# Rotary embedding, fp32: 64 rows of x to a partition, table halves made by TensorE and VectorE, x staged in PSUM by ScalarE

## Chip, cores, metric

One core of one Trainium2 chip. The metric is the device time of one execution in microseconds (us); lower is better. The *span* of a profile runs from the first to the last instruction that it shows. It is shorter than the measured time, that difference here called the **gap**.

## The reference

x is (8, 8, 1024, 64) in fp32, 16.8 MB; the tables are (1024, 32) each.

```python
half = x.shape[-1] // 2
x_first, x_second = x[..., :half], x[..., half:]
out_first  = x_first * cos_cached - x_second * sin_cached
out_second = x_first * sin_cached + x_second * cos_cached
return np.concatenate([out_first, out_second], axis=-1)
```

Each row needs two products over its 64 elements (by sin and by cos) and two sums over 32. Everything is read once and written once: 33.8 MB of transfers with the tables.

## The kernel before

x is cut into 16 chunks of 128 partitions x 32 rows (8 KB a partition). The tables lie in SBUF (for GpSimd) and in PSUM (for VectorE). VectorE makes the products of most chunks; the sums are made by GpSimd (`vector_pool`), by TensorE with the identity and its negative plus a copy back by ScalarE (`vector_tensor`), or by VectorE (`vector_alone`). Two chunks are GpSimd's alone.

```python
R = 32; F = R * hd; T = R * half; Q = seq // R        # 32 partitions hold one table
for first, n in [(0, 1), (1, 1)] + [(c, 2) for c in range(2, n_ch, 2)]:
    t = xp.tile([P, n, F], fp32, name=f"x{first}")    # all of x fits in SBUF
    nc.sync.dma_start(out=t, in_=xf[first:first + n].rearrange("c p m -> p c m"))
# ... identity `plus` on GpSimd, `minus` on ScalarE
for r in range(reps):                                 # tables to PSUM, four times
    nc.vector.tensor_copy(out=snp[r * Q:(r + 1) * Q], in_=sn[0:Q])
    nc.scalar.copy(out=csp[r * Q:(r + 1) * Q], in_=cs[0:Q])
for t in (sn, cs):                                    # and in SBUF for GpSimd
    for r in range(1, reps):
        nc.gpsimd.tensor_copy(out=t[r * Q:(r + 1) * Q], in_=t[0:Q])

def products(eng, c, s, ctab, stab):
    xr = rows(xt[c])
    eng.tensor_tensor(out=rows(s), in0=xr, in1=tab(stab), op=TT.mult)
    eng.tensor_tensor(out=xr, in0=xr, in1=tab(ctab), op=TT.mult)
# ... vector_tensor(0); on_pool(1); vector_pool(2); ... vector_alone(15)
```

## Time and profile before

| | before |
|---|---|
| measured time, median of 4 runs | 85.98 us (85.87 to 86.01) |
| span of the profile | 84.2 us |
| gap between time and span | 1.8 us |
| busy: VectorE, GpSimd, ScalarE | 84%, 85%, 19% of the span |
| moved | 33.82 MB in 4736 packets |

A kernel that is bound by its transfers gets faster only by moving its bytes more cheaply or by making the ramp and the tail shorter.

### The profile page before, as it was taken

What the parts mean: (1) busy time and instruction counts of PE and PEld (TensorE: products, weight loads), DVE (VectorE), ACT (ScalarE), POOL (GpSimd) and SP (SyncE); (2) the same over time, 40 slices, a digit from 0 to 9 for tenths busy, and PEclk for the clock granted to TensorE, in tenths of its full rate; (3) what the DMA queues carried; (4) which work ended last, traced back from release to release, by engine and by line L of the source; (5) the groups of instructions that cost most, each with busy time, mean ns of one, the idle gap of its engine ahead of it and who ended that gap; (6) DMA issues with size and microseconds to landing.
All of it is one profiled execution on the core that took longest, in us unless ns stands there. A gap on an engine that the chain in (4) does not pass through costs nothing.

```text
span 84.2 us, 363 instructions
## 1 busy us (share of the span) xinstructions
PE 40.1 (48%) x80; PEld 15.7 (19%) x80; DVE 70.4 (84%) x34; ACT 15.7 (19%) x16; POOL 71.4 (85%) x38
## 2 busy tenths in 40 slices
PE   0000005994930896895949497794949600000000
PEld 0000002422400341423314051332414100000000
DVE  0199997999999999999999982999999999996000
ACT  4399000004040003104040402204040310000000
POOL 3199999999999999999999999999999999970000
PEclk9999999999999569999999999999999999555555
DMA  3899999999999999999999999999999999999991
GB/s 29 282 432 409 420 420 436 417 409 420 436 428 409 417 428 432 432 424 409 421 436 436 432 421 417 424 424 436 432 432 432 413 421 428 428 436 407 432 419 55
DMA packets 4736, 33.82 MB, mean 402 GB/s; under 512 B 448, under 2 KB 448, under 8 KB 768
## 3 DMA queue, kind: packets, MB, share of 16 engines
q1 hardware_dynamic: 3824, 27.40, 78.7%
q10 hardware_dynamic: 912, 6.42, 18.1%
HBM read 17.04 MB, written 16.78 MB: 402 GB/s over the span
## 4 chain that ended last, share of the span: by engine, by line
POOL 53%; DVE 23%; issue 9%; DMA 4%; DVEq 1%; POOLq 0%
POOL x L94 13%; POOL x L93 11%; DVE vs L88 11%; POOL x L89 11%; POOL gs L88 11%; DVE x L89 8%; POOL sn L77 4%; DMA sn<-in_sin_cached_dram 4%; POOL cs L77 3%; DVE acc L88 3%; DVE x L93 1%; DVEq L170 1%; POOLq L93 0%; POOLq L77 0%
## 5 line engine op out<-in xcount | busy, mean ns | idle before, releaser
L119 PE MATMUL acc<-x,plus 128*128 128x512 f32 x40 | 23.3, 666 | 26.4 <-DVE x L89 13.6
L89 DVE TENSOR_TENSOR x<-x,csp 128x2048 f32<-128x2048 f32 x14 | 32.0, 2287 | 0.6
L88 DVE TENSOR_TENSOR vs<-x,snp 128x2048 f32<-128x2048 f32 x13 | 29.7, 2282 | 2.2 <-POOL x L94 1.7
L122 ACT COPY x<-acc 128x1024 f32<-128x1024 f32 x10 | 10.1, 1012 | 49.2 <-PE acc L120 49.2
L94 POOL TENSOR_TENSOR x<-x,vs 128x1024 f32<-128x1024 f32 (+1 forms) x9 | 19.0, 2108 | 0.0
L93 POOL TENSOR_TENSOR x<-x,vs 128x1024 f32<-128x1024 f32 (+1 forms) x9 | 18.9, 2105 | 0.0
L119 PEld LDWEIGHTS acc<-x,plus 128*128 128x128 f32 x40 | 7.5, 208 | 39.4 <-issue 23.9
L120 PE MATMUL acc<-vs,minus 128*128 128x512 f32 x20 | 11.6, 666 | 0.0
L120 PE MATMUL acc<-vs,plus 128*128 128x512 f32 x20 | 10.2, 592 | 0.0
L89 POOL TENSOR_TENSOR x<-x,cs 128x2048 f32<-128x2048 f32 x2 | 9.1, 4546 | 0.2
L88 POOL TENSOR_TENSOR gs<-x,sn 128x2048 f32<-128x2048 f32 x2 | 9.1, 4542 | 0.1
L73 DVE COPY snp<-sn 32x1024 f32<-32x1024 f32 x4 | 4.9, 1223 | 3.9 <-DMA sn<-in_sin_cached_dram 3.8
L120 PEld LDWEIGHTS acc<-vs,minus 128*128 128x128 f32 x20 | 4.4, 219 | 5.9 <-issue 5.9
L77 POOL COPY sn<-sn 32x1024 f32<-32x1024 f32 x3 | 3.1, 1032 | 2.7 <-DMA sn<-in_sin_cached_dram 2.6
L93 POOL TENSOR_TENSOR x<-x,gs 128x1024 f32<-128x1024 f32 x2 | 4.7, 2362 | 0.2
L94 POOL TENSOR_TENSOR x<-x,gs 128x1024 f32<-128x1024 f32 x2 | 4.7, 2357 | 0.0
L120 PEld LDWEIGHTS acc<-vs,plus 128*128 128x128 f32 x20 | 3.8, 190 | 4.8 <-issue 4.8
L74 ACT COPY csp<-cs 32x1024 f32<-32x1024 f32 x4 | 4.0, 1008 | 1.5 <-DMA cs<-in_cos_cached_dram 1.4
L77 POOL COPY cs<-cs 32x1024 f32<-32x1024 f32 x3 | 3.1, 1033 | 0.1
L88 DVE TENSOR_TENSOR acc<-x,snp 128x2048 f32<-128x2048 f32 x1 | 2.3, 2297 | 0.0
L71 ACT ACT_TABLE_LOAD x1 | 1.3, 1283 | 1.2 <-PEq L159 1.2
L93 DVE TENSOR_TENSOR x<-x,acc 128x1024 f32<-128x1024 f32 x1 | 1.2, 1223 | 0.0
(8 smaller groups left out, 2.4 us busy)
## 6 DMA issues: line engine op xcount, KB each, us to landing
x<-in_x_dram SPq DMA_DIRECT2D x7, 2048.0 KB, 25.0
out_dram<-x SPq DMA_DIRECT2D x9, 1024.0 KB, 13.0
out_dram<-x ACTq DMA_DIRECT2D x6, 1024.0 KB, 9.0
x<-in_x_dram SPq DMA_DIRECT2D x2, 1024.0 KB, 6.3
out_dram<-x SPq DMA_DIRECT2D x2, 512.0 KB, 6.0
cs<-in_cos_cached_dram ACTq DMA_DIRECT2D x1, 128.0 KB, 3.4
sn<-in_sin_cached_dram SPq DMA_DIRECT2D x1, 128.0 KB, 3.1
```

What stands on the lines that cost most here:

```text
L71: nc.scalar.mul(minus, plus, -1.0)
L73: nc.vector.tensor_copy(out=snp[r * Q:(r + 1) * Q], in_=sn[0:Q])
L74: nc.scalar.copy(out=csp[r * Q:(r + 1) * Q], in_=cs[0:Q])
L77: nc.gpsimd.tensor_copy(out=t[r * Q:(r + 1) * Q], in_=t[0:Q])
L88: eng.tensor_tensor(out=rows(s), in0=xr, in1=tab(stab), op=TT.mult)
L89: eng.tensor_tensor(out=xr, in0=xr, in1=tab(ctab), op=TT.mult)
L93: eng.tensor_tensor(out=xr[:, :, 0], in0=xr[:, :, 0], in1=sr[:, :, 1], op=TT.subtract)
L94: eng.tensor_tensor(out=xr[:, :, 1], in0=xr[:, :, 1], in1=sr[:, :, 0], op=TT.add)
L119: nc.tensor.matmul(a[:, k], plus, xr[:, :, k], start=True, stop=False)
L120: nc.tensor.matmul(a[:, k], plus if k else minus, sr[:, :, 1 - k], start=False, stop=True)
L122: nc.scalar.copy(out=xr, in_=a.rearrange("p k n j -> p n k j"))
L170: with _tile.TileContext(nc) as tc:
```

## The change

The intent: longer contiguous runs of x (16 KB a partition) in fewer and larger transfers, and less table work at the start. With 64 rows to a partition, a partition needs table rows of two neighbouring blocks of 32. The even blocks are spread over 128 partitions by a selection matrix on TensorE; the odd ones are shuffled by VectorE into 32 partitions and copied to the rest. From the second half of unit 0 on, the tables lie in SBUF only, so ScalarE copies x to PSUM ahead of VectorE's products, which keeps VectorE at one SBUF input.

```diff
-    R = 32
+    R = 64                                   # F and T double; 8 units, not 16 chunks
+    for m0, m1 in ((0, F // 2), (F // 2, F)):
+        nc.sync.dma_start(out=xt[0][:, m0:m1], in_=xf[0][:, m0:m1])
+    for u in range(1, n_u):
+        nc.sync.dma_start(out=xt[u], in_=xf[u])             # 16 KB a partition
...
-    for r in range(reps):
-        nc.vector.tensor_copy(out=snp[r * Q:(r + 1) * Q], in_=sn[0:Q])
-        nc.scalar.copy(out=csp[r * Q:(r + 1) * Q], in_=cs[0:Q])
+        for i in range(2):                                  # even blocks
+            for part, r in zip(even, (rs, rc)):
+                nc.tensor.matmul(part[i], sel, r[:, i * BK:(i + 1) * BK], start=True, stop=True)
+        odd = [2 * (i % (Q // 2)) + 1 for i in range(Q)]    # odd blocks
+        for t, r in ((sn, rs), (cs, rc)):
+            nc.vector.stream_shuffle(t[0:Q, C:], r, odd)
+        # ... three copies each on ScalarE and GpSimd; even blocks copied to SBUF by ScalarE
...
+    def stage(pt, u, n0, n1):
+        nc.scalar.copy(out=pt[:, :(n1 - n0) * hd], in_=xt[u][:, n0 * hd:n1 * hd])
+    def products(pt, u, n0, n1, alone=False):
+        mul(nc.vector, sr, pr, tab(sn, n0, n1))             # pr: x in PSUM
+        mul(nc.vector, pr if alone else xr, pr, tab(cs, n0, n1))
...
+    # unit 2 is GpSimd's; units 1, 3 to 7 go in chunks of 24, 24 and 16 rows:
+    for c, (u, n0, n1) in enumerate(chunks):
+        products(st[c % 2], u, n0, n1, (u, n0) in alone)
+        put(c + 2)                                          # stage two chunks ahead
+        # ... TensorE's sums back, next TensorE sums, GpSimd's sums, stores of whole units
```

## The prediction

> **What bounds the kernel now.** I read three views in this order: the strip of 40 slices, the table of busy time in chosen windows, then the groups and the chain that ended last. First the strip, with the DMA rows under the engines' rows:
>
> ```profile
> DVE  0199997999999999999999982999999999996000
> POOL 3199999999999999999999999999999999970000
> DMA  3899999999999999999999999999999999999991
> GB/s 29 282 432 409 420 420 436 417 409 420 436 428 409 417 428 432 432 424 409 421 436 436 432 421 417 424 424 436 432 432 432 413 421 428 428 436 407 432 419 55
> DMA packets 4736, 33.82 MB, mean 402 GB/s; under 512 B 448, under 2 KB 448, under 8 KB 768
> ```
>
> VectorE and GpSimd look full, but both stop three to four slices before the end. The DMA row is full from the third slice to the 39th. A slice is 2.1 us, so only the ramp (1.5 us idle in the first slice) and the last receipt (about 1.9 us) are without traffic. Second, the windows (columns: length, busy of PE, PEld, DVE, ACT, POOL, then clock, DMA share, GB/s):
>
> ```profile
> 10.00:20.00 10.00, 5.38 (x8) 2.08 (x8) 9.42 (x5) 0.93 (x1) 9.76 (x4) 1.00 1.02 424
> 60.00:65.00 5.00, 3.90 (x10) 1.47 (x9) 4.96 (x3) 1.01 (x1) 4.97 (x3) 1.00 1.01 428
> 75.00:80.00 5.00, 0.00 (x0) 0.00 (x0) 2.19 (x2) 0.00 (x0) 0.30 (x1) 0.50 1.03 428
> 80.00:82.00 2.00, 0.00 (x0) 0.00 (x0) 0.00 (x0) 0.00 (x0) 0.00 (x0) 0.50 0.96 408
> ```
>
> The rate is the same while loads run, while stores run, and after all compute is over (80 to 82 us). The transfers set the end. The chain view blames POOL (53%) and DVE (23%), but it follows one store's data back and does not see that this store stood in a backlog. VectorE's last sum starts at 75.97 us and takes 1.21, the last store is issued at 77.22, and the span ends at 84.2. Third, the groups that the change touches:
>
> ```profile
> L89 DVE TENSOR_TENSOR x<-x,csp 128x2048 f32<-128x2048 f32 x14 | 32.0, 2287 | 0.6
> L122 ACT COPY x<-acc 128x1024 f32<-128x1024 f32 x10 | 10.1, 1012 | 49.2 <-PE acc L120 49.2
> L94 POOL TENSOR_TENSOR x<-x,vs 128x1024 f32<-128x1024 f32 (+1 forms) x9 | 19.0, 2108 | 0.0
> L89 POOL TENSOR_TENSOR x<-x,cs 128x2048 f32<-128x2048 f32 x2 | 9.1, 4546 | 0.2
> L73 DVE COPY snp<-sn 32x1024 f32<-32x1024 f32 x4 | 4.9, 1223 | 3.9 <-DMA sn<-in_sin_cached_dram 3.8
> L93 DVE TENSOR_TENSOR x<-x,acc 128x1024 f32<-128x1024 f32 x1 | 1.2, 1223 | 0.0
> ```
>
> These are my prices: a VectorE product over 2048 elements 2.29 us, over 1024 1.22; a ScalarE copy of 1024 elements 1.01; GpSimd per 2048 elements 4.55. Vector instructions overlap a little: the timeline shows two products every 4.52 us (starts at 18.52, 23.04, 27.56), so I use 2.13 us of work plus 0.08 to 0.18 of overhead each.
>
> **What the Trainium skill says.** "DMA: Bandwidth & Descriptors", section Bandwidth, "Where 436 GB/s comes from", puts the ceiling at 435.2 GB/s; the strip agrees, no slice is above 436. The same page, "Why small descriptors are slow", says that a packet pays a fixed cost beside its bytes. The trace agrees: in its packet records an 8192-byte packet takes 309 ns (313 to 314 while loads run) and a 4096-byte one 159, which is 9 ns plus 150 for each 4 KB. "SBUF — State Buffer", "Who interferes with whom", says that a VectorE instruction with at most one SBUF input does not contend with GpSimd. The trace agrees: products with one operand in PSUM stay at 2.28 to 2.29 us with GpSimd busy beside them. The new form, x in PSUM and the table in SBUF, also has one SBUF input, so I keep the price. "VectorE: DVE Perf Modes", the perf-mode tier table, gives a shuffle some 2400 ns for 2048 elements; my estimate for 1024 is thus 1.2 us. No run here shows one yet.
>
> **The change part by part.**
>
> *Transfers.* Bytes stay the same, but runs get longer. Now each of the 16 engines moves about 248 packets of 8 KB (32 MB less the 256 half-store packets, so 3968 / 16), 20 of 4 KB and 28 completions: 248 x 0.309 + 20 x 0.159 + 28 x 0.009 = 80.1 us. After: loads are 16 packets of 8 KB (unit 0 in halves) and 56 of 16 KB; stores are 56 of 16 KB, 8 of 12 KB, 8 of 4 KB; tables 4 of 4 KB; 20 completions. By the 9 + 150 ns rule a 16 KB packet is 609 ns and a 12 KB one 459: 16 x 0.309 + 112 x 0.609 + 8 x 0.459 + 12 x 0.159 + 20 x 0.009 = 78.9 us. **The saving is 1.15 us, and it is on the path**, because the path is the DMA. That a 16 KB run stays one packet is assumed.
>
> *Start.* Removed: four VectorE copies (4.9 us), four ScalarE copies (4.0), and three of GpSimd's six copies of 1.03. Added: four selection matmuls into PSUM beside two shuffles. Shuffles run from 3.84 us (sin table landed) to 6.2. The first product needs the first 1 MB of x: the first three slices have moved 0.06 + 0.59 + 0.91 = 1.56 MB at 6.3 us, of which 0.26 are tables, so it is there at about 6.3. The first product starts at 6.4 and not at 8.87: **2.4 us earlier for VectorE**, but no transfer waits for it, since loads fill the queue until about 45 us. Worth nothing by itself.
>
> *VectorE.* Unit 0: 8 products of 1024 at 1.14 = 9.1 us, to 15.5. Unit 1 lands near 14 us (before, the 2 MB load behind the same 2 MB released VectorE at 13.99); its first 24 rows are staged by ScalarE in 1.46 (1.5 x 1.01, less overhead), so about 15.5: hardly a wait. Six units, each four products of 1536 at 1.68 and two of 1024 at 1.14: 9.0, together 54. Own sums are 72 rows where there were 32, eight instructions, 4608 elements: 4.8 plus 8 x 0.1 and some 1.2 for in-place dependences, 6.8 us. End 15.5 + 54 + 6.8 = 76.3; I allow 0.7 where unit 3's load shares the engines with the first store. **VectorE ends near 77**, where it ended before (77.2): the shorter start pays for the extra sums.
>
> *GpSimd.* Table copies to 8.2; three pairs of sums of unit 0, 2.5 us each, to about 19; unit 2 whole, 2 x (9.1 + 4.7) = 27.6, to 46.8; units 3, 4, 5 at 4.6 each; 48 rows of unit 6 done by 68.2; 24 rows of unit 7 by about 72. It has waits of its own now and is not the bound.
>
> *ScalarE.* 15.7 us become about 41: staging 6 x (2 x 1.46 + 1.01) = 23.6 plus 2 for unit 0, 10.1 for the ten copies back, table copies and loads the rest. It has room: a chunk's staging of 1.46 lies inside VectorE's 3.35 for the other buffer.
>
> *Does the DMA stay fed?* Stores of 2 MB come in larger lumps, each 4.9 us of transfer. Stores 0 and 1 are issued near 21 and 38 us; loads plus these two last until about 51. Then, ready against needed: store 2 at 47 for 51, store 3 at 51.5 for 56, store 4 at 57 for 61, store 5 at 64 for 66, store 6 at 69 for 71, the first 48 rows of store 7 at 72 for 75.5, the last 16 at 76.5 to 77 for 79. Each is ahead by 2 to 4 us, so I expect no hole. Sum: 84.2 - 1.15 = 83.0 us of span, and 85.97 - 1.15 = **84.8 us**.
>
> **The rivals.**
>
> *A: packets do not get longer or cheaper.* If 16 KB runs are cut at 8 KB, nothing on the path changes: 85.9 to 86.1 us. No record here is above 8192 bytes, but none of the runs is longer either, so the profile cannot tell.
>
> *B: compute becomes the bound.* VectorE has 22 more instructions, each dependent on staging by ScalarE, whose queue also holds copies back that wait for PE (3.8 us for a group). Every 3.5 us chunk that waits 0.3 us adds up to 5 us. A lone last store of 0.5 MB costs about 4 us after VectorE's end (a 128 KB table took 3.1 to land, plus some 0.9 for the extra bytes), so the end passes 83.0 only if VectorE ends after about 79. For it: chunks are finely interleaved and store 5 and 6 lead by only 2 us. Against: ScalarE busy half the time. If so, 86 to 88 us.
>
> *C: more comes of it than packet overhead,* for instance if the 313 ns packets of the load phase become nearer 300 per 8 KB. At the ceiling of 435 GB/s the 33 MB of the full slices would take 75.9 us and not 77.9: 2 us, and 84.0 us. The strip's maxima of 436 are no evidence: they are counts of whole packets in a slice.
>
> **Range and chances.** Main line 84.8; A gives 86.0, C about 84.0, B up to 88. The 2% mark is 84.25, which the main line misses by half a microsecond, so faster needs C or a better tail. I give the main line and A together 0.74, C 0.18, B past 2% slower 0.08. The range is 84.0 to 86.3.
>
> **What would show it.** Right: packets fall from 4736 to about 2700, full slices read near 430 instead of 424 GB/s, the DMA row stays at 9 to the 39th slice, VectorE's first product starts near 6.4 and its work ends near 77, products of 1536 take about 1.75 us and shuffles about 1.2. Wrong: packets above 4500 (rival A); a digit below 9 in the DMA row after slice 22, with VectorE ending after 79 and waiting for ScalarE's staging (rival B); shuffles or PSUM products much longer than priced; a 16 KB packet clearly under 609 ns (rival C).

## The result

The changed kernel takes **87.14 us** (median of 4 runs, 86.86 to 87.57) against 85.98: ratio 1.014, 95% interval 1.010 to 1.018. Within 2%, but outside the predicted 84.0 to 86.3, and on the other side of the kernel before. A ratio here is the mean time of one kernel's fast runs over that of the other's of the same rounds, so not quite the ratio of the medians.

The same rows of the page, after:

```profile
span 84.5 us, 434 instructions
...
DVE  0299879999999999999999999999999999990000
ACT  4368895804371955695197635560875671000000
POOL 5059019999999999999999999999979999300000
...
DMA  2999898999999999999999999999999999999980
GB/s 33 316 403 489 380 489 380 481 388 465 396 427 318 365 427 442 419 450 396 465 396 465 396 473 396 458 411 427 442 419 450 411 454 411 450 419 421 427 357 10
DMA packets 2690, 33.83 MB, mean 400 GB/s; under 512 B 320, under 2 KB 320, under 8 KB 512
...
q14 instruction: 2, 0.02, 0.1%
```

Much is as predicted: 2690 packets, a DMA row of 9 in nearly every slice (8 in the fifth, the seventh and the 39th), engines that stop before the end. The single slices swing more (380 to 489, but for two low ones at 25 to 30 us and the last full one) because the page counts a 16 KB packet in one slice. The last line is new: two packets of *instructions* were fetched within the span, where the page of before has no such line. The timeline of VectorE, start and end:

```profile
3.69 1.28 DVE L138 STREAM_SHUFFLE sn<-raw 32x1024 f32<-32x1024 f32 x1
6.43 1.22 DVE L84 TENSOR_TENSOR s<-x,n 128x1024 f32<-128x1024 f32 x1 [0.20 <-DMA x<-in_x_dram]
75.45 0.68 DVE L88 TENSOR_TENSOR x<-st,s 128x512 f32<-128x512 f32 x1
76.16 0.34 ACTq L120 DMA_DIRECT2D out_dram<-x  x1
```

The first product starts at 6.43 us (predicted 6.4), the last store is issued at 76.16, a microsecond before that of the old kernel (77.22). Yet the span is 84.5 in this profile and 84.2 on average of the four runs (84.0 to 84.5), and not 83.0. The windows of both kernels, before first, then after (the last two columns are the DMA share and GB/s):

```profile
10.00:24.00 14.00, 9.08 (x16) 3.52 (x16) 13.38 (x7) 1.14 (x2) 13.76 (x5) 1.00 1.02 424
24.00:30.00 6.00, 2.26 (x3) 1.17 (x4) 5.93 (x4) 0.88 (x1) 6.00 (x4) 0.78 1.00 418
30.00:66.00 36.00, 28.28 (x62) 10.97 (x60) 34.02 (x16) 7.08 (x7) 35.81 (x15) 0.99 1.01 426
82.00:82.40 0.40, 0.00 (x0) 0.00 (x0) 0.00 (x0) 0.00 (x0) 0.00 (x0) 0.50 0.78 328
82.40:82.80 0.40, 0.00 (x0) 0.00 (x0) 0.00 (x0) 0.00 (x0) 0.00 (x0) 0.50 0.01 0
```

```profile
10.00:24.00 14.00, 6.86 (x11) 2.53 (x10) 13.52 (x11) 7.73 (x9) 11.64 (x7) 1.00 1.01 431
24.00:30.00 6.00, 4.90 (x12) 1.95 (x11) 5.97 (x6) 3.80 (x3) 5.84 (x3) 1.00 1.03 377
30.00:66.00 36.00, 26.76 (x56) 10.27 (x55) 35.97 (x27) 21.68 (x19) 35.30 (x14) 0.95 1.01 431
82.00:82.40 0.40, 0.00 (x0) 0.00 (x0) 0.00 (x0) 0.00 (x0) 0.00 (x0) 0.50 0.49 195
82.40:82.80 0.40, 0.00 (x0) 0.00 (x0) 0.00 (x0) 0.00 (x0) 0.00 (x0) 0.50 0.11 41
82.80:83.20 0.40, 0.00 (x0) 0.00 (x0) 0.00 (x0) 0.00 (x0) 0.00 (x0) 0.50 0.03 10
```

The rate in full stretches did rise, to 431 GB/s. There is a dip from 24 to 30 us; and at the end a few packets are still moving when most are done (41 GB/s is about a tenth of the full rate), where in the profile of before all ended nearly together. These are single executions: the kernel's second profile (r1, span 84.0) moves 10 GB/s from 82.4 to 82.8 us, and two profiles of the kernel before with additions (r2, r5) move 41 there.

Against the kernel before, the loss is not in the span at all: the average is 84.2 for both. Measured time less span is 1.7 to 1.9 us in every run of the kernel before for which I have both, and 2.9 to 3.1 in the four runs of this one. The DMA view of the changed kernel from 84.4 us on, after the last instruction of the span, has

```profile
q8 instruction: 1, 0.02, 1.4%
q14 instruction: 1, 0.01, 0.4%
```

where the same view of the kernel before is empty (0 packets).

So three questions: what is outside the span, what are longer packets worth, and what happens in the dip and at the end?

### The profile page after: what moved, and what is told of

Read it like the earlier page. It is cut to its first block, busy times and chain, and to the rows that moved or that the text cites. A ratio compares the mean times of both kernels' runs of the same rounds, so it can differ in the third digit from the quotient of the medians.

```text
span 84.5 us, 434 instructions
## 1 busy us (share of the span) xinstructions
PE 47.7 (56%) x88; PEld 18.2 (22%) x88; DVE 71.2 (84%) x56; ACT 41.7 (49%) x39; POOL 63.6 (75%) x37
## 2 busy tenths in 40 slices
DMA packets 2690, 33.83 MB, mean 400 GB/s; under 512 B 320, under 2 KB 320, under 8 KB 512
## 3 DMA queue, kind: packets, MB, share of 16 engines
q1 hardware_dynamic: 2208, 28.97, 82.4%
## 4 chain that ended last, share of the span: by engine, by line
DVE 47%; issue 2%; ACT 1%; DVEq 1%
DVE s L84 20%; DVE x L84 17%; DVE st L84 5%; DVE x L87 2%; DVE x L88 2%; ACT st L98 1%; DVEq L239 1%
## 5 line engine op out<-in xcount | busy, mean ns | idle before, releaser
L98 ACT COPY st<-x 128x1536 f32<-128x1536 f32 (+1 forms) x18 | 23.4, 1304 | 13.3 <-DVE x L84 10.2
L84 DVE TENSOR_TENSOR s<-st,sn 128x1536 f32<-128x1536 f32 (+1 forms) x18 | 28.3, 1574 | 0.0
L84 DVE TENSOR_TENSOR x<-st,cs 128x1536 f32<-128x1536 f32 (+1 forms) x14 | 22.9, 1638 | 0.0
L87 POOL TENSOR_TENSOR x<-x,s 128x512 f32<-128x512 f32 (+2 forms) x9 | 16.3, 1809 | 4.4 <-issue 4.0
L88 POOL TENSOR_TENSOR x<-x,s 128x512 f32<-128x512 f32 (+2 forms) x9 | 16.3, 1808 | 0.0
L168 PE MATMUL acc<-s,minus 128*128 128x512 f32 x20 | 12.0, 685 | 0.0
L168 PE MATMUL acc<-s,plus 128*128 128x512 f32 x20 | 10.2, 592 | 0.0
L84 POOL TENSOR_TENSOR g<-x,sn 128x2048 f32<-128x2048 f32 x2 | 9.1, 4552 | 0.1
L84 DVE TENSOR_TENSOR st<-st,cs 128x1024 f32<-128x1024 f32 (+1 forms) x4 | 5.4, 1361 | 0.0
L168 PEld LDWEIGHTS acc<-s,minus 128*128 128x128 f32 x20 | 4.2, 212 | 5.3 <-issue 5.3
L87 POOL TENSOR_TENSOR x<-x,g 128x1024 f32<-128x1024 f32 x2 | 4.7, 2358 | 0.2
L88 POOL TENSOR_TENSOR x<-x,g 128x1024 f32<-128x1024 f32 x2 | 4.7, 2340 | 0.0
```

What stands on the lines that cost most here:

```text
L84: eng.tensor_tensor(out=o, in0=a, in1=t, op=TT.mult)
L87: eng.tensor_tensor(out=o[:, :, 0], in0=c[:, :, 0], in1=s[:, :, 1], op=TT.subtract)
L88: eng.tensor_tensor(out=o[:, :, 1], in0=c[:, :, 1], in1=s[:, :, 0], op=TT.add)
L98: nc.scalar.copy(out=pt[:, :(n1 - n0) * hd], in_=xt[u][:, n0 * hd:n1 * hd])
L168: nc.tensor.matmul(a[:, k], plus if k else minus, sr[:, :, 1 - k], start=False, stop=True)
```

## The experiments

The kernels ran beside runs of the kernel before. Spans are given as means over a kernel's runs.

| run | span, this / before | gap, this | time, median | ratio (95%) |
|---|---|---|---|---|
| r1 changed kernel again | 84.2 / 84.2 | 2.1 to 2.9 | 86.70 | 1.009 (1.004 to 1.015) |
| r2 before + 32 ScalarE copies | 84.2 / 84.2 | 1.8 | 86.00 | 1.000 (0.998 to 1.002) |
| r3 before + 32 VectorE copies | 84.8 / 84.2 | 1.8 | 86.62 | 1.007 (1.006 to 1.009) |
| r4 before + one shuffle | 84.0 / 84.2 | 1.8 | 85.88 | 0.999 (0.997 to 1.000) |
| r5 before + 6 matmuls | 84.3 / 84.2 | 1.8 to 2.0 | 86.15 | 1.002 (0.999 to 1.004) |
| r6 before + all three paddings | 84.5 / 84.2 | 1.7 to 1.9 | 86.41 | 1.005 (1.003 to 1.006) |
| r7 changed, shorter TensorE program | 84.7 / 84.2 | 2.1 to 2.2 | 87.02 | 1.013 (1.011 to 1.015) |
| r8 before, 16 KB runs | 85.1 / 84.2 | 1.8 | 86.89 | 1.010 (1.009 to 1.012) |
| r9 before + 5 GpSimd fills | 84.0 / 84.2 | 2.1 to 2.2 | 86.14 | 1.002 (1.001 to 1.004) |
| r10 changed, shorter GpSimd program | 84.2 / 84.2 | 2.0 to 2.9 | 86.60 | 1.009 (1.006 to 1.012) |
| r11 r10 with 8 KB runs | 84.6 / 84.2 | 1.8 to 2.2 | 86.69 | 1.009 (1.007 to 1.011) |
| r12 changed, both programs shorter | 84.4 / 84.2 | 1.8 to 1.9 | 85.87 | 1.000 (0.996 to 1.004) |
| r13 before + fills + 9 matmuls | 84.0 / 84.2 | 2.1 to 2.5 | 86.25 | 1.002 (0.998 to 1.007) |
| r14 before + 5 matmuls | 84.1 / 84.2 | 1.7 to 2.2 | 85.93 | 1.001 (0.999 to 1.003) |
| r15 changed + one matmul | 84.3 / 84.2 | 1.9 to 2.2 | 86.33 | 1.004 (1.003 to 1.006) |
| r16 r10 + one matmul | 84.4 / 84.2 | 2.0 to 3.5 | 87.07 | 1.013 (1.010 to 1.016) |

(One run of r12, 87.11, and two of r13, 87.36 and 87.12, are slow and left out of these rows; with them the medians are 86.31 and 86.90. Of r13 two fast runs remain. The result of r8 is wrong; those of the other runs are correct.)

### Is it repeatable, and is it ScalarE's or VectorE's program, or the shuffle?

Theory: the engines' programs have grown, and some late fetch of instructions costs time outside the span. Rival: the shuffle instruction does. r1 repeats the changed kernel; r2 to r4 add to the kernel *before*, in idle time of the engine:

```diff
+    for _ in range(32):                       # r2, after ScalarE's table copies
+        nc.scalar.copy(out=junk, in_=plus[:, 0:32])
+    for _ in range(32):                       # r3, after VectorE's last sum
+        nc.vector.tensor_copy(out=junk, in_=plus[:, 0:32])
+    nc.vector.stream_shuffle(junk[0:32, :], plus[0:32, 0:32], odd)   # r4, same place
```

> The changed kernel again, unaltered. In its first profile the load packets that arrived from 25.7 to 27.9 us took about 1000 ns instead of 611, before any packet of the second store queue, and this cost about 0.9 us of transfer. Theory hole-is-systematic: the same slices (about 24 to 30 us) again read 320 to 370 GB/s where the others read about 430, and the span is again 84.0 to 84.5. Theory hole-is-chance: in this profile the slices at 24 to 30 us read about 430 GB/s, or the dip lies at another time. Beside this, theory outside-the-span: the measured time exceeds the profiled span by 2.9 to 3.1 us again, where the kernel before has 1.8.

> The kernel before with 32 tiny copies (128x32) more on ScalarE, in time in which ScalarE has nothing to do (8 to 19 us). Theory program-length-of-ScalarE: the changed kernel pays some 1.2 us outside the span because ScalarE's program has grown from about 40 to about 69 instructions and part of it has to be fetched late; then this kernel has a span of 84.2 as before but a measured time about 1.2 us more, 87.2, and the page shows instruction packets on queue 14. Rival (another engine's program, or the shuffle): 86.0, with the gap between time and span still 1.8.

> The kernel before with 32 tiny copies (128x32) more on VectorE after its last sum, where it has about 5 us of slack before the transfers end. Theory program-length-of-VectorE: its program has grown from about 48 to about 71 instructions in the changed kernel, and that costs 1.2 us outside the span; then this kernel measures about 87.2 with a span of 84.2. Rival (another engine, or the shuffle): 86.0 with a gap of 1.8.

> The kernel before with one tiny 32x32 shuffle more on VectorE after its last sum, its result unused. Theory shuffle: use of this instruction, and of the mask load that goes with it, brings the 1.2 us outside the span; then this kernel measures about 87.2 with a span of 84.2. Rival (program length): 86.0 with a gap of 1.8.

r1: the dip came back (343 GB/s in one slice), and so did a large gap, between 2.1 and 2.9. But the strips of r2, r3 and r4 show the dip as well, 284, 359 and 348 GB/s in the slice at 27 to 29 us, though they move 8 KB packets, and their spans are those of the kernel before, or longer for another reason. The dip is therefore no property of the change; that the only profile of the kernel before has none may be chance. Its cause stays open. In the packet records its lowest microsecond ends within 0.7 us of the first packet of the second store queue (q10, ScalarE's) in all 16 of the 18 profiles that have a dip, wherever that packet lies: at 24.7 us in r7 and r12, 27.7 to 30.2 in most, 35.5 in r13. Of the two without one, r8 has its first such packet only at 52.3; the kernel before has it at 28.5 and still no dip.

r2, r3 and r4 all keep the gap at 1.8: neither ScalarE's nor VectorE's length alone, nor the shuffle. r3's span is longer because the 32 copies take 6.86 us and carry VectorE to 83.9 us, past the end of the transfers; I had taken them for cheaper.

### TensorE's program, all three together; and packets alone

```diff
+    for _ in range(6):                        # r5, r6: between the tables and the first sums
+        nc.tensor.matmul(acc[:, 0:512], plus[0:Q, :], sn[0:Q, 0:512], start=True, stop=True)
```

r7 takes away in the changed kernel: `pool_sums(0, 0, G)` in place of TensorE's group for those 16 rows. r8 gives the kernel before the runs of the change, with wrong tables:

```diff
-        "(c p m) -> c p m", p=P, m=F)
+        "(u p m) -> u p m", p=P, m=2 * F)     # chunk c: half c % 2 of unit c // 2; one store a unit
```

> The kernel before with six fp32 matmuls more on TensorE at the start (into the accumulator before it is used, between 4 and 13 us, when TensorE has nothing else to do), so that its program is about as long as in the changed kernel. Theory program-length-of-TensorE (the last engine whose program grew): span 84.2 as before, but the measured time exceeds the span by about 2.5 to 3 us instead of 1.8, so about 87.0. Rival (what is outside the span comes only when the programs of several engines are long, or of something else): 86.0 and a gap of 1.8.

> The kernel before with ScalarE, VectorE and TensorE all padded in idle time to about the instruction counts of the changed kernel (29 and 23 tiny copies, six matmuls), transfers untouched. Theory sum-of-programs (all engines' late instruction fetches together put the last one behind the end of the span): span 84.2 to 84.6 and a gap of 2.1 to 3.1 us, so 86.5 to 87.3. Rival (the gap comes from something that the changed kernel does other than having more instructions): gap 1.8, time 86.0 to 86.4.

> The changed kernel with one of its ten TensorE groups (the first 16 rows of unit 0) given to GpSimd, which is idle then, so that TensorE's program has as many matmuls as before. Result still correct. Theory program-length-of-TensorE: gap between measured time and span back to 1.8, time about 85.9, span 84.0 to 84.3 unchanged. Rival: gap still 2.1 to 3.1, time 86.3 to 87.2.

> The kernel before with only the memory layout of the change: 64 rows of x to a partition for loads and for stores (a store for each pair of chunks, the last pair in its old pieces), tables left as they are, so the result is wrong on purpose; compute and program lengths are unchanged or shorter. Prediction's rule (9 ns a packet saved): 1.1 us less, 84.9. Rival from the overlap of packets in the traces (a full slice moves 427.2 GB/s with 8 KB and 431.5 with 16 KB packets, 1.0 per cent): 0.7 us less, 85.3. Rival larger packets save nothing at the end because the engines finish less evenly: 85.7 to 86.0. The gap outside the span should stay at 1.8 in all three.

r5 and r6 keep the gap at 1.7 to 2.0, so these three lengths are not enough. r6 tells something else: its span is 84.53 against 84.19, although its last store is issued at 77.04 us, as before. The page counts two fetched instruction packets within the span, as in the changed kernel, and the tail is uneven: 62 GB/s still moved from 82.4 to 82.8 us, where the kernel before moved nothing. But r5 moved 41 there without any such packet.

r7's gap was a steady 2.1 to 2.2, between the two kernels: part of it is gone. r8 went wrong as a test of packets, and shows instead what lumps cost:

```profile
64.00:66.00 2.00, 2.00 (x6) 0.86 (x5) 2.00 (x2) 0.00 (x0) 2.00 (x2) 1.00 1.11 475
66.00:68.00 2.00, 0.64 (x2) 0.00 (x0) 1.97 (x2) 1.01 (x1) 2.00 (x1) 1.00 0.44 188
68.00:70.00 2.00, 0.00 (x0) 0.00 (x0) 2.00 (x1) 0.00 (x0) 2.00 (x2) 0.94 0.94 393
```

Here *engines* are the DMA engines: stores of whole units in the old order leave them short of work at 66 us, since the store issued at 58.2 us lands at 68.0 and the next is issued only at 67.8. The changed kernel, with whole units in a new order, has no such hole in its profile; that the order is the reason was not tested apart. 16 KB stores aren't free of charge.

### GpSimd's program, and packets again

r9 adds five fills on GpSimd at the start of the kernel before. r10 shortens GpSimd's program in the changed kernel from 66 entries of the built list to 62; r11 is r10 with all loads and stores cut in two, so that packets are 8 KB again and all else stays.

```diff
-    nc.gpsimd.memset(sel, 0.0)                # r10, r11, r12, r16
-    nc.gpsimd.affine_select(out=s3, in_=s3, ...)
-    nc.gpsimd.memset(plus, 0.0)
+    nc.vector.memset(plus, 0.0)
+    nc.vector.tensor_copy(out=sel..., in_=pick.to_broadcast(...))    # every second column of plus
```

> The kernel before with five tiny fills more on GpSimd at the very start, in time that it waits for the tables: its program has 68 entries in the built list instead of 63 (the changed kernel has 66). Padding the other three engines left the gap between measured time and span at 1.7 to 2.0 us. Theory program-length-of-GpSimd (its last block of instructions is fetched only after the span's end): span 84.2, gap 2.1 to 3.1 us, time 86.3 to 87.3. Rival (the gap belongs to something else in the changed kernel): gap 1.8, time 86.0.

> The changed kernel with the selection matrix taken from the identity by VectorE at the start and one fill moved there too, so that GpSimd's program has 62 entries instead of 66; nothing on the path changes, result correct. Theory program-length-of-GpSimd: gap back to 1.8 us, span 84.0 to 84.5 as before, time 85.8 to 86.3, thus level with the kernel before. Rival: gap 2.1 to 3.1 and time 86.3 to 87.5 as for the changed kernel.

> The kernel of the run before this with every load and store cut into 8 KB runs again (two instructions for one), result correct; GpSimd's program has 65 entries. Compare spans, not times, with the run before this. My prediction's rule (9 ns for each 8 KB packet more): span 1.1 us longer. Full-slice rates of the traces so far (427.2 against 431.5 GB/s): 0.7 us longer. Rival, that 16 KB packets gain in the middle and give it back in the uneven finish of the engines (last engine 0.6 us behind the median one with 16 KB, 0.2 to 0.35 with 8 KB): 0.0 to 0.4 us longer. If the gap is GpSimd's program, 65 entries tell whether the limit lies below or above that.

r9 is a clear answer for a part: gap 2.10 to 2.17 in four of four runs, 0.35 us above the kernel before, from five fills that cost the span nothing. (The spans of r9 are 0.17 us shorter than those of the kernel before, so the measured time rose by 0.17 only; a ratio of 1.002.) Its DMA view after the end of the span shows

```profile
DMA packets 1, 0.01 MB, mean 2 GB/s; under 512 B 0, under 2 KB 0, under 8 KB 0
...
q14 instruction: 1, 0.01, 0.8%
```

**So a longer GpSimd program brings an instruction packet behind the span and a gap larger by 0.35 us.** The other profiles agree about the packet: a q14 packet lies behind the span in all seven profiles in which GpSimd has 64 to 67 entries (the trace counts one less than the built list), and in none of the eleven with 61 or 62. That the program's end waits for this packet is likely, not shown. And in r10, whose profile has none (gap 2.09), the gap was still 2.0 to 2.1 in three runs and 2.7 to 2.9 in three, so there is more.

r10 and r11 are the test of the packets. Windows from 30 to 66 us, each from its own profile, r10 first:

```profile
30.00:66.00 36.00, 26.38 (x55) 10.15 (x54) 35.97 (x26) 21.25 (x19) 35.26 (x14) 0.95 1.01 431
```

```profile
30.00:66.00 36.00, 26.46 (x59) 10.38 (x58) 35.97 (x27) 22.55 (x20) 35.31 (x14) 1.00 1.01 428
```

VectorE's busy time is the same; the rate differs by 0.7%. The span is 84.23 against 84.63 on average of six runs each: **16 KB packets are worth 0.40 us, not 1.15.** That is at the upper end of the lowest of the three expectations. It holds for packets and transfers together: r11 also issues nearly twice as many transfers (560 completion packets for 320).

### Both programs, and what remains

r12 shortens GpSimd's program to 63 entries and TensorE's by the group of r7; r13 lengthens both in the kernel before.

> The changed kernel with both programs shortened: GpSimd's to 63 entries (one fill, the selection matrix and one table copy moved to VectorE and ScalarE, which have time there) and TensorE's to 58 (one group of sums given to GpSimd). Shortening TensorE alone (58) left a steady gap of 2.15 us, shortening GpSimd alone (62) one of 2.0 to 2.1 in half the runs and 2.7 to 2.9 in the other half. Theory two-programs (GpSimd's late fetch is 0.35 us of the gap, TensorE's the rest): gap 1.8 us in all runs, and with a span of 84.0 to 84.3 a time of 85.8 to 86.1. Rival (a third thing): gap 2.1 or more. The span of the run with TensorE shortened stood at 84.0 once and at 84.8 to 85.0 four times; if that comes from the moved sums, it is seen here again and the time is 86.6 to 86.8.

> The kernel before with GpSimd padded by five fills (68 entries, as in the run that gave a gap of 2.1 us) and TensorE by nine matmuls (63 entries, as in the changed kernel), both in idle time. Theory two-programs: gap 2.7 to 3.1 us in some or all runs, time 86.7 to 87.2 at a span of 84.2. Rival (TensorE's length is not it): gap 2.1 us as with GpSimd alone, time 86.2.

r12's gap is 1.77 to 1.87 in six of six runs. With the five of r7 that makes eleven runs without TensorE's tenth group and none with an additional piece beyond GpSimd's 0.35. But r13 brought it in one of its two fast runs only (2.48; the other 2.11). And r11, with all ten groups, doesn't have it either: 1.83 to 2.19 in six runs. So the tenth group alone doesn't decide. The span of r12's fast runs fell in two groups, 83.9 to 84.1 and 84.9 to 85.1, as r7's did. The profile was of a long one (windows, then one line of ScalarE's timeline):

```profile
58.00:60.00 2.00, 2.00 (x3) 0.67 (x2) 2.00 (x2) 0.38 (x1) 2.00 (x2) 0.50 0.97 418
60.00:62.00 2.00, 1.16 (x3) 0.25 (x1) 2.00 (x3) 0.80 (x1) 1.53 (x1) 0.95 1.11 475
62.00:64.00 2.00, 1.74 (x4) 0.87 (x5) 2.00 (x2) 1.55 (x3) 0.36 (x1) 1.00 0.68 287
```

```profile
61.20 1.01 ACT L171 COPY x<-acc 128x1024 f32<-128x1024 f32 x1 [2.83 <-PE acc L167]
```

The copy back of unit 4's sums starts only at 61.20, so its store cannot go before 62.2, and the DMA engines run dry (287 GB/s). In the changed kernel's profile that copy starts at 59.45 and the store is ready at 60.5, half a microsecond ahead of the 61 at which my list has the queue run out. Its lead is thus thin too; in its eight runs the span stayed at 84.0 to 84.5.

TensorE's granted clock is 0.50 from 58 to 60 us, but that is not what differs: the changed kernel has such a stretch too, at 55.0 to 58.4 us, and its copy waits as long for TensorE (2.82 against 2.83 us). r12's execution has one more, from 39.7 to 43.1 us, here in one window (r12 first, then the changed kernel; the clock is the third number from the end):

```profile
39.00:43.00 4.00, 4.00 (x7) 1.49 (x6) 4.00 (x4) 1.02 (x1) 3.93 (x1) 0.59 0.98 422
39.00:43.00 4.00, 3.15 (x8) 1.12 (x6) 4.00 (x4) 1.83 (x2) 3.92 (x2) 1.00 1.01 434
```

The copy back behind it starts at 44.11 after a wait of 3.58 us for TensorE, against 42.18 and 1.89, and the later ones stay 1.75 us or more behind. The profile of r7, a short run with the same group taken from TensorE, has one stretch and that copy at 42.34. But each is one profile; the long runs of r7 have none, and why r12's has the second stretch is open.

r14 to r16 asked whether the *place* where TensorE's program ends decides, by adding matmuls: five at the start of the kernel before, one at the very end of the changed kernel and of r10.

```diff
+    nc.tensor.matmul(acc[:, 0:P], plus, plus, start=True, stop=True)   # r15, r16; nobody reads it
```

> The kernel before with five matmuls more on TensorE: 192 entries in TensorE's two rows of the trace, one less than the 193 of the changed kernel (six matmuls gave 196 and a gap of 1.8 to 2.0, nine gave 208). Theory boundary (a late fetch costs only where TensorE's program ends just past a block's edge, and 193 is such a length): gap 1.8 if the edge lies at 193, or 2.0 to 2.9 if it lies a little below. Rival (not TensorE's length at all): gap 1.8. So only a larger gap decides here.

> The changed kernel with one matmul MORE on TensorE at the very end, into an accumulator that nobody reads: 197 entries for 193, result correct, GpSimd still long. Theory boundary (TensorE's program ends just past the edge of a block that is fetched at the end; a few entries more and it is fetched earlier, hidden): gap falls to 2.1 to 2.2 us, GpSimd's part alone, though the program got longer; time 86.2 to 86.5. Rival (the sums that the shorter program no longer did, not its length): gap stays at 2.1 to 3.1 as for the changed kernel, median near 2.9.

> The same matmul more, in the changed kernel with GpSimd's program trimmed to 62 entries. Theory boundary: gap 1.8 us in all runs, span 84.1 to 84.4, time 85.9 to 86.2, level with the kernel before. Rival: gap 2.0 to 2.9, as without the additional matmul.

r15 did as the edge theory wants (gap 1.9 to 2.2), r16 did the opposite (2.0 to 3.5), r14 was 1.7 to 1.8 in three runs and 2.2 in one. The theory of an edge is not upheld. What the profiles do show: a 16 KB instruction packet on queue 8 after the span's end, in five of them, those of the changed kernel (both), r14, r15 and r16, all with a longer TensorE program. That is not sufficient: r5, r6, r10, r11 and r13 have a longer one too, and no such packet. Where there is one, the gap goes with its time: it starts 2.26, 1.77, 1.26, 0.38 and 0.37 us after the span's end (changed kernel, r1, r14, r15, r16), and the gaps of these executions are 3.07, 2.53, 2.20, 2.07 and 2.08. Whether the end waits for this packet or both wait for something else, what triggers it, and why its time varies between runs of one kernel, stays open.

## Why the prediction was wrong

- **Bound: right.** The transfers set the end of the span before and after.
- **Start and VectorE: right.** First product predicted at 6.4, measured at 6.43; VectorE's end near 77, measured 76.1; shuffles 1.2, measured 1.28 and 1.34; products of 1536 elements 1.75, as measured; ScalarE's busy time about 41, measured 41.7. Nothing contradicts that the earlier start is worth nothing by itself; no run tested it alone. One reading was off, without use in the sum: the last receipt is not about 1.9 us, since the last data packet ends at 82.70 us of a span of 84.16.
- **"The saving is 1.15 us, and it is on the path": mechanism right, size wrong.** The number of packets was right (2690), and a 16 KB packet takes 611 ns in the records, close to the predicted 609. But the rule took recorded durations for time spent. Packets overlap a little: the share column of the windows read 1.01 to 1.02 before, which 16 engines with one packet each at a time cannot reach. In the packet records from 30 to 66 us, 16.16 packets are open at once on average before and 16.08 after. The overhead that I saw was partly hidden already. The term measures 0.40 us (r11 less r10): 0.75 missing.
- **A term that the sum did not have: what the rest of the change costs the span.** With 8 KB packets (r11) the changed kernel's span is 0.46 us longer than that of the kernel before (84.63 against 84.17). Its source is not settled. r6 shows that longer programs alone lengthen the span, by 0.34 us, with transfers and the issue of the last store as before; an uneven tail goes with it. Two instruction packets within the span, 309 ns each in the records, are a possible way. Against it: one such packet (r2) cost nothing visible, the profiles of r1 and r7 have two at a span of 84.0, r5 has an uneven tail without any, and which engine carried them the trace does not tell. So this is a guess.
- **"85.97 - 1.15 = 84.8": the step that failed most.** It carried the gap of 1.8 us over from the kernel before. The changed kernel's gap is 2.8 us on average of eight runs. Of that additional 1.0 us, GpSimd's longer program is some 0.35 (shown by r9 on the kernel before; the changed kernel without that length, r10, has 0.4 less on average, but never less than 2.03). The rest goes away when TensorE's program loses one group (r7, r12), but also with ten groups in r11 and r15 (1.8 to 2.2), by a mechanism that is not settled.
- Together: 84.8 + 0.75 + 0.46 + 1.0 = 87.0, against medians of 87.14 and 86.70. The last two terms are measured, their causes mostly not known.
- **Rival A** is out (packets did get longer). **Rival B** did not happen here, but my list of leads was too generous: store 4 was to be ready at 57 for 61, and was ready at 60.5; r12's profile shows a later copy turn this into a hole. **Rival C** is out too: the rate rose by less than the fixed cost says, not by more.

No version beats the kernel before clearly: r12 in its short runs takes 85.7 to 85.9, r4 85.88.

## What to carry to other kernels

When the transfers are saturated, price a change by the measured rate of full stretches at both packet sizes, not by the difference of single packet durations, and ask how evenly the engines finish. Compare measured time less span as well as the span: five more fills on GpSimd added a third of a microsecond to that difference (half as much to the time) that no row of the page shows, while 32 more copies on ScalarE or VectorE added none. Larger stores need more lead, since one late copy then holds back 2 MB (r12). And where a profile is of one execution, look at a second before explaining its tail or its dip.

## What the Trainium skill lacked or had wrong

- "Runtime: NRT & Kernel Launch", Instruction fetch mechanics, says that crossing a block of the instruction stream costs "one DMA tail-bump, mostly hidden". r9 bears this out only in part: five more instructions on GpSimd bring one fetch behind the kernel's last instruction, with 0.35 us more outside the span and 0.17 us more of measured time. The page names blocks of 16 KiB; most instruction packets here are of 8 KB.
- "DMA: Bandwidth & Descriptors", Bandwidth, has the fixed cost per packet for small descriptors only, and no page has what 8 against 16 KB are worth: 428 and 431 GB/s in full stretches, 0.40 us in 84.
- The same page does not say how far the recorded durations of packets overlap (a share of 1.01 to 1.02), so that they can't be summed.
- No page has the dip before the second store queue's first packet: 284 to 359 GB/s in one slice of 2.1 us (r1 to r4), in kernels with 8 and 16 KB packets.
